# Low parts of six weight tiles formed by accumulating transfers, and one mean placed later, between the two layers of a hybrid encoder

## The chip, the core and the metric

The kernel runs on one core of a Trainium2 chip. The metric is the device time of one execution in microseconds (us). The core has a tensor engine (PE), VectorE (DVE), ScalarE (ACT), GpSimd (POOL) and a sync engine (SP) that issues most loads.

## The reference

Two layers of a bidirectional encoder over 512 tokens of 1024 channels, in float32. Each layer has two sub-layers, and each of these normalises its input and its output (RMS norm) and adds the output to the residual stream `x`:

```python
for l in range(DEPTH):                      # DEPTH = 2
    h = rms_norm(x, g_pre_mix[l])
    proj = h @ w_in[l]                      # 1024 -> 5632
    q_a, k_a, v_a, q_b, k_b, v_b, q_m, gate_pre = jnp.split(proj, splits, axis=-1)
    ...
    o_m = memory_attention(q_m, mem_n, w_mem_kv[l])   # keys and values: mem_n @ w_mem_kv[l]
    ...
    x = x + rms_norm(merged @ w_out[l], g_post_mix[l])
    h = rms_norm(x, g_pre_ffn[l])
    u = depthwise_conv_centred(h @ w_up[l], conv_w[l], conv_b[l])
    a, b = jnp.split(u, 2, axis=-1)
    x = x + rms_norm((jax.nn.gelu(a) * b) @ w_down[l], g_post_ffn[l])
```

`rms_norm(y, g)` is `y * rsqrt(mean(y*y) + 1e-6) * g`, the mean over the 1024 channels.

## The kernel before, in words

Channels lie on the 128 partitions, in `KD` = 8 groups; tokens lie along the free dimension, in two halves of 256 (`HALVES`). A float32 product is made of three matmuls in the type fp32r: each operand is split into a high part (a copy rounded to fp32r) and a low part (the operand minus its high part), and `mm3` (lines 249 to 254) adds high x high, weight high x operand low, and weight low x operand high. The weight's low part is thus wanted by the third of the three.

`weights` (lines 227 to 244) loads a weight tile of 128 output channels, 128x1024 elements or 512 KB, through SP into one of three buffers `wraw`. With a slot given, the tile is split in two chunks of 128x512: `split` (lines 223 to 225) lets ACT copy the chunk into the high part and lets the engine `eng` subtract that from the raw chunk into the low part. `eng` is VectorE (`V`) unless the caller names GpSimd (`G`). The buffer `wraw` is free when both have read it. The high and low parts of such tiles come from the pool of tiles called `m` (32 of them), so that in the profile ACT's copies read `m<-wraw` and the subtractions `m<-wraw,m`.

PE's order is written out by hand. `Woven` keeps a planner's clock that counts a cost for each matmul (a matmul of 256 columns counts 0.107 us), ties every PE instruction behind the one before, and holds a heap of jobs. A job is a generator: `yield t` makes it due again t us of the planner's clock later, `yield "flag"` parks it. `tick`, called after each step of `linear` or `run_group`, runs the jobs that are due, so the number in a `yield` decides behind how many matmuls the job's next PE instruction stands. `need(flag)` runs jobs until a flag is given.

Between the layers these things run side by side:

- `sublayer_end` of layer 0 (lines 815 to 862) ends the channel-mixing product for half 0, then for half 1. For half 0 it spawns `end_job` (lines 379 to 392): the reciprocal root of the mean square (`rstd_job`: PE multiplies the summed squares `acc` by the column `mean`, ACT takes the root, VectorE the reciprocal, PE transposes it back), then for each of eight channel groups `y = y * r`, `x = x + y`, and the squares of `x` summed into `acc2`. Then comes the next layer's `pre_norm_job`, which begins with the mean of `acc2` and writes the normalised tiles `h`.
- For half 1 it spawns `raw_end_job` (lines 418 to 445): the same, but each `x` is first split unnormalised (`raw`), so that PE can begin on it, and the mean of `acc2` (the yield of line 436 stands ahead of it) gives the factors `R`, by which the products are multiplied afterwards (lines 908 to 911), and the tiles `h` of half 1.
- `kv_ahead` (lines 1013 to 1023) loads and splits four key/value tiles of the next layer (`KVE`, line 38, names the engine for 1, 2 and 3) and the first two of the six tiles of the first projections (`GEN`, one letter for each of the six in `FIRST`). The other four follow at line 1029. `mem_kv` (lines 479 to 492) multiplies the key/value tiles; `run_group` (lines 501 to 514) multiplies the six tiles in three pairs, first by half 0, then by `raw`: the pairs' banks are called mm and mm, o and pt, s and s in the profile. Tiles 2 and 3 of the group (counted from 0) make the pair o and pt, tiles 4 and 5 the pair s and s.

With `KVE` = 'VVGG' and `GEN` = 'GGVGVG', six tiles are subtracted by GpSimd: key/value tiles 2 and 3, and tiles 0, 1, 3 and 5 of the group, in two chunks each.

GpSimd also runs, in this stretch, copies of the memory keys (`twice_split`), and for each attention head the load of its bias table and three subtractions (`a_bias`, lines 593 to 600). That load is tied behind `last_lo.get(G)`, the last low part that `split` gave to GpSimd.

Of the kernel before, what the change touches and what calls it, by code (L numbers as in the profile page):

```python
# [10 lines left out]
ALU = mybir.AluOpType  # L11
# [9 lines left out]
KD = D_MODEL // 128  # L21
# [6 lines left out]
FIRST = (0, 3, 4, 7, 6, 1)  # L28
# [6 lines left out]

LAT_QK, LAT_SM, LAT_T, LAT_V, LAT_T2 = 1.0, 4.5, 1.5, 2.0, 0.6
STEP_A, STEP_B, STEP_M = 9.0, 9.0, 5.5
SQG, LOG, GEN, KVE = {0: (), 1: ()}, {0: (), 1: ()}, 'GGVGVG', 'VVGG'
SD1 = 4.0
MARGIN = 0.3  # L40
SB = True
# [1 line left out]
KVD, GWD, NG, LAT1 = 7.3, 1.0, 2, 12.0  # L43
# [76 lines left out]
def tile_hybrid_encoder(ctx, tc, xT, memT, memg, vecs, rpb, w_in, w_kv, w_bra, w_brb, w_brm,  # L120
                        w_out, w_up, w_down, c_ident, c_mask, c_tab0, c_tab1, out):
    nc = tc.nc
# [13 lines left out]
    uid, last_copy, last_act, crit, last_lo = [0], [None], [None], [None], {}  # L136
    wv = Woven(tc)

    def nm(s):
        uid[0] += 1  # L140
        return f"{s}_{uid[0]}"


    def big(dt=F32R, shape=(128, 512)):
        return mp.tile(list(shape), dt, tag="m", name=nm("m"))
# [4 lines left out]
    def ktile(dt=F32R, shape=(128, 512)):  # L150
        return tp.tile(list(shape), dt, tag="ka", name=nm("ka"), bufs=12)
# [22 lines left out]
    def f32(ap):  # L174
        return ap.bitcast(F32)

    G = nc.gpsimd
    ACT, V = Counted(nc.scalar, wv, 0.1, 0.8e-3), Counted(nc.vector, wv, 0.065, 1.05e-3)

    DUP, MDUP = G, G  # L180
    MSQ = G

    def ready(least):
# [5 lines left out]
    def xh(k, half):  # L189
        return xs[:, half.start // 256, k, :]  # L190
# [27 lines left out]
    def behind(ins, other):  # L218

        if other is not None and ins is not other:  # L220
            tc.add_manual_dep(ins, other.name, ORDER, reason="issue order")

    def split(src, hi, lo, eng=None):
        last_copy[0] = ACT.copy(hi, src).ins
        last_lo[eng or V] = (eng or V).tensor_sub(lo, src, f32(hi)).ins

    def weights(src, K, C, slot=None, eng=None, after=None):

        raw = wp.tile([128, K, C], F32, tag="wraw", name=nm("wraw"))
        nc.sync.dma_start(out=raw, in_=src)  # L230
        if slot is None:
            hi = wp.tile([128, K, C], F32R, tag="whi", name=nm("whi"), bufs=2)
            lo = wp.tile([128, K, C], F32R, tag="wlo", name=nm("wlo"), bufs=2)
            split(raw, hi, lo, eng)
            behind(last_copy[0], after)
            return [(hi[:, k, :], lo[:, k, :]) for k in range(K)]
        n = 512 // C
        w = []
        for k in range(0, K, n):
            c = min(n, K - k)  # L240
            hi, lo = slot(F32R, (128, c, C)), slot(F32R, (128, c, C))
            split(raw[:, k:k + c, :], hi, lo, eng)
            w += [(hi[:, i, :], lo[:, i, :]) for i in range(c)]
        return w

# [68 lines left out]
    def sumsq_add(acc, src, first, slot=None, eng=None):  # L314
        if first:
            ACT.activation(acc, src, AF.Square)
        else:
            n = acc.shape[-1]
            sq = slot((128, 256)) if slot else small("sq2", 4) if n == 256 else small("sq", 1, (128, 512))
            ACT.activation(sq, src, AF.Square)  # L320
            (eng or V).tensor_add(acc, acc, sq)
# [4 lines left out]
    def rstd_job(accs, n, box):  # L326

        nb = n // 128
        bank = tbank((128, n + nb))
        pr, pt = bank[:, 0:n], bank[:, n:n + nb]  # L330
        for i, a in enumerate(accs):
            for b in range(nb):
                mm(pt[:, b:b + 1], a[:, 128 * b:128 * b + 128], mean, i == 0 and b == 0,
                   i == len(accs) - 1 and b == nb - 1, 0.11)
        rs = smalls(nb)
        crit[0] = ACT.activation(rs, pt, AF.Sqrt, bias=eps, scale=1.0).ins
        V.reciprocal(rs, rs)
        yield 0.8
        for b in range(nb):
            one = rs[:, b:b + 1]  # L340
            spread = bass.AP(one.tensor, one.offset, [list(one.ap[0]), [0, 128]])
            wv.pe(nc.tensor.transpose(pr[:, 128 * b:128 * b + 128], spread, ident), 0.11)
        box.append(pr)

    def normed(src, g, rs, hi, lo, eng=None):
        h32 = small("h32", 3)
        V.scalar_tensor_tensor(out=h32, in0=src, scalar=g, in1=rs, op0=ALU.mult, op1=ALU.mult)
        split(h32, hi, lo, eng)

    def raw_split(l, goff, k, src, hi, lo):  # L350

        g = vec[:, l, goff + k:goff + k + 1]
        ACT.activation(hi, src, AF.Copy, scale=g)
        V.scalar_tensor_tensor(out=lo, in0=src, scalar=g, in1=f32(hi), op0=ALU.mult, op1=ALU.subtract)

    def rtile():
        return tp.tile([128, 512], F32, tag="R", name=nm("R"), bufs=1)
# [60 lines left out]
    def raw_end_job(l, goff, og, acc, acc2, nxt, lat):  # L418


        half, box = HALVES[1], []
        hs, raw, R = nxt
        yield lat
        raw.extend((t[:, 0, :], t[:, 1, :]) for t in [ktile(F32R, (128, 2, 256)) for _ in range(KD)])
        yield from rstd_job([acc[:, half]], 256, box)
        for k in range(KD):
            V.tensor_mul(og[k][:, half], og[k][:, half], box[0])
            V.tensor_add(xh(k, half), xh(k, half), og[k][:, half])
            raw_split(l + 1, V_PRE, k, xh(k, half), *raw[k])
            if k == 0:  # L430
                yield 0.6
            wv.give(f"raw{k}")
            yield 1.05
        for k in range(KD):
            sumsq_add(acc2[:, half], xh(k, half), k == 0)
        yield 3.5
        box = []
        yield from rstd_job([acc2[:, half]], 256, box)
        ACT.copy(R[:, half], box[0])
        wv.give("R")  # L440
        for k in range(KD):
            normed(xh(k, half), vec[:, l + 1, V_PRE + k:V_PRE + k + 1], box[0], hs[k][0][:, half], hs[k][1][:, half])
        crit[0] = last_copy[0]
        yield 1.2
        wv.give(f"h{l + 1}.{V_PRE}.1")

    def h_tiles():
        return [(htile(), htile()) for _ in range(KD)]


    def mem_norm_job(l, hm, slot):
# [6 lines left out]
        for k in range(KD):  # L458
            sumsq_add(acc, raws[k], k == 0, None, MSQ if l else V)
        yield 14.0  # L460
# [34 lines left out]
    def group_weights(srcs, engs):  # L495
        return [weights(s, KD, 128, big, e) for s, e in zip(srcs, engs)]
# [19 lines left out]
    def proj(l, m, hs, after=None):  # L516
        w = weights(w_in[l, m], KD, 128, after=after)
        ps = mmbank()
        linear(ps, w, hs)
        return ps  # L520
# [366 lines left out]
    gw = group_weights([w_in[0, m] for m in FIRST[:2]], (V, V))  # L887
# [14 lines left out]
    for l in range(depth):  # L902
# [41 lines left out]
        for m in range(KD):  # L944
# [3 lines left out]
            hi, lo = big(), big()  # L948
# [4 lines left out]
        hs, R, gw = h_tiles(), rtile(), []  # L953
# [44 lines left out]
        if l == depth - 1:  # L998
            sublayer_end(l, V_POSTF, w_of, fs, 2, None)
            while wv.jobs:  # L1000
                wv._step()
        else:
            hm, km, vm = [], [], []
            wv.spawn(mem_norm_job(l + 1, hm, htile), 20.0)
            pre, R, raw, box = [], rtile(), [], []

            def then(a, i, l=l, box=box):
                box.extend(h_tiles())
                return pre_norm_job(l + 1, V_PRE, a, box, i)

            gw = []

            def kv_ahead(l=l, pre=pre, gw=gw):
                pre.append(weights(w_kv[l + 1, 0], KD, 128, htile))
                yield KVD
                for i in (1, 2, 3):
                    yield 0.9
                    pre.append(weights(w_kv[l + 1, i], KD, 128, big, G if KVE[i] == 'G' else V))
                wv.give(f"kv{l + 1}")
                for m in range(NG):  # L1020
                    yield GWD
                    gw.extend(group_weights([w_in[l + 1, FIRST[m]]], [G if GEN[m] == 'G' else V]))
                wv.give(f"gw{l + 1}")

            sublayer_end(l, V_POSTF, w_of, fs, 1, [then, (box, raw, R)], (1.4, LAT1), lambda: wv.spawn(kv_ahead()))
            wv.need(f"kv{l + 1}")
            mem_kv(l + 1, hm, km, vm, pre)
            wv.need(f"gw{l + 1}")
            gw += group_weights([w_in[l + 1, m] for m in FIRST[NG:]], [G if e == 'G' else V for e in GEN[NG:]])
            wv.need(f"h{l + 1}.{V_PRE}.0")  # L1030
            hs = box

# [92 lines left out]
```

## Time and profile before

| what | us |
|---|---|
| median of 3 runs | 1551.7 |
| lowest of them | 1549.61 |
| the profiled execution | 1551.73 |
| its span in the profile | 1550.0 |

The page of the profile gives busy times, the span in 40 slices, the DMA queues, the chain that ended last, and the costliest groups of instructions. The trace behind it was asked for waits, for timelines of one engine, for groups of one shape and for the granted clock of short stretches. Times of a timeline count from the span's start. A name such as `mm<-h,m` is output<-inputs, without buffer numbers; L114 is the helper through which all ACT and VectorE instructions pass, L247 the matmul of `mm`, L225 the subtraction of `split`, L342 the transposes of `rstd_job`.

### The profile page before, as it was taken

The page shows a single profiled execution, that of the slowest core. Times are in us where ns is not written, and L with a number is a line of the kernel's source. Part 1 is how long each engine was busy: PE and PEld are TensorE (multiplying, and loading weights), DVE is VectorE, ACT ScalarE, POOL GpSimd, SP SyncE. Part 2 cuts the span into 40 slices and gives each one's busy share as a digit, 9 for nine tenths or more (in the row PEclk, how much of TensorE's full clock was granted, in tenths as well). Part 3 has the DMA queues.
Part 4 walks back from the last instruction along what each step waited for, and adds up shares of the span by engine and source line. Part 5 has one row for each costly group of instructions (what it writes and reads, how often), then busy time and mean ns, then how long its engine had stood idle before and what let it go on. Part 6 is the DMA issues. An engine that isn't in the chain of part 4 may idle for free.

```text
span 1550.0 us, 20648 instructions
## 1 busy us (share of the span) xinstructions
PE 1522.5 (98%) x7970; PEld 1300.1 (84%) x7970; DVE 951.6 (61%) x1684; ACT 712.7 (46%) x1266; POOL 149.7 (10%) x217
## 2 busy tenths in 40 slices
PE   8999999999999999999989999999999999999997
PEld 7988888888988888888888888888889888888887
DVE  6685676335777777742497756753456977776233
ACT  5565554336544444532355555532354544444231
POOL 3340000110000000000154300002100000000000
PEclk9999999999999999999999999999999999999999
DMA  7221213235113322333431221132350233323331
GB/s 246 89 88 64 62 57 107 84 95 165 53 59 100 100 96 95 118 90 101 129 102 59 78 66 58 61 104 88 102 177 15 82 96 99 101 99 89 99 105 63
DMA packets 45810, 144.91 MB, mean 93 GB/s; under 512 B 5376, under 2 KB 9600, under 8 KB 45712
## 3 DMA queue, kind: packets, MB, share of 16 engines
q1 hardware_dynamic: 43776, 139.85, 28.5%
q10 hardware_dynamic: 1296, 2.10, 0.4%
q0 software_dynamic: 640, 1.64, 0.3%
q8 instruction: 62, 1.02, 0.3%
q14 instruction: 36, 0.29, 0.1%
HBM read 141.48 MB, written 2.10 MB: 93 GB/s over the span
## 4 chain that ended last, share of the span: by engine, by line
PE 91%; DVE 6%; ACT 2%; issue 1%; DMA 0%; SPq 0%; ACTq 0%; DVEq 0%
PE mm L247 80%; PE s L247 4%; PE o L247 3%; PE pt L258 2%; DVE m L114 1%; DVE y L114 1%; PE pt L247 1%; DVE ka L114 1%; DVE x L114 1%; ACT y L114 1%; DVE st L114 0%; DVE acc L114 0%; DMA x<-in_xT_dram 0%; DVE wlo L114 0%; ACT whi L114 0%
## 5 line engine op out<-in xcount | busy, mean ns | idle before, releaser
L247 PE MATMUL mm<-h,whi 128*128 128x512 f32 x2496 | 776.5, 392 | 0.0
L247 PEld LDWEIGHTS mm<-h,whi 128*128 128x128 f32 x2496 | 462.0, 188 | 91.3
L247 PE MATMUL mm<-h,wlo 128*128 128x512 f32 x1248 | 486.9, 390 | 0.0
L114 DVE TENSOR_TENSOR wlo<-wraw,whi 128x1024 fp32r<-128x1024 f32 (+1 forms) x213 | 259.2, 1217 | 284.7 <-ACT whi L114 282.3
L114 ACT CAST whi<-wraw 128x1024 fp32r<-128x1024 f32 (+1 forms) x213 | 221.4, 1040 | 307.8 <-PE mm L247 293.4
L247 PEld LDWEIGHTS mm<-h,wlo 128*128 128x128 f32 x1248 | 234.5, 188 | 49.6
L247 PE MATMUL mm<-m,whi 128*128 128x512 f32 (+1 forms) x800 | 215.1, 356 | 1.0 <-DVE m L114 0.8
L247 PEld LDWEIGHTS mm<-m,whi 128*128 128x128 f32 x800 | 141.8, 189 | 22.8 <-PE mm L247 1.3
L247 PE MATMUL mm<-m,wlo 128*128 128x512 f32 (+1 forms) x400 | 142.1, 355 | 0.0
L114 DVE SCALAR_TENSOR_TENSOR y<-y,vec,y 128x511 f32<-128x511 f32 x176 | 130.5, 748 | 3.5 <-ACT y L114 0.9
L114 DVE TENSOR_TENSOR y<-mm,R 128x512 f32<-128x512 f32 x82 | 56.4, 688 | 68.5 <-PE mm L247 68.5
L247 PEld LDWEIGHTS mm<-m,wlo 128*128 128x128 f32 x400 | 75.5, 189 | 10.9
L802 POOL TENSOR_TENSOR m<-m,y 128x512 f32<-128x512 f32 x28 | 36.1, 1289 | 399.4 <-DVE y L114 399.4
L114 ACT ACTIVATE y<-y,vec 128x512 f32<-128x512 f32 x88 | 71.1, 815 | 2.3 <-DVE y L114 1.9
L247 PE MATMUL mm<-m,m 128*128 128x512 f32 x240 | 63.5, 394 | 0.0
L114 ACT ACTIVATE y<-y 128x512 f32<-128x512 f32 x44 | 27.9, 633 | 71.7 <-DVE y L114 71.3
L114 ACT CAST m<-pt 128x512 fp32r<-128x512 f32 (+1 forms) x72 | 38.6, 541 | 46.8 <-PE pt L258 38.5
L114 ACT ACTIVATE y<-y,st 128x256 f32<-128x256 f32 (+1 forms) x80 | 43.8, 549 | 30.4 <-DVE st L114 28.9
L114 DVE TENSOR_TENSOR acc<-acc,sq 128x256 f32<-128x256 f32 (+1 forms) x80 | 41.1, 514 | 26.6 <-ACT sq L114 24.7
L114 DVE TENSOR_TENSOR m<-pt,m 128x512 fp32r<-128x512 f32 (+1 forms) x72 | 45.1, 630 | 19.9 <-ACT m L114 18.6
L114 ACT CAST m<-y 128x512 fp32r<-128x512 f32 x32 | 19.9, 622 | 72.5 <-DVE y L114 72.5
L247 PE MATMUL mm<-h,m 128*128 128x256 f32 x312 | 49.1, 301 | 2.0 <-ACT h L114 1.0
(154 smaller groups left out, 1789.9 us busy)
## 6 DMA issues: line engine op xcount, KB each, us to landing
wraw<-in_w_in_dram SPq DMA_DIRECT2D x88, 512.0 KB, 3.7
wraw<-in_w_up_dram SPq DMA_DIRECT2D x88, 512.0 KB, 3.6
wraw<-in_w_down_dram SPq DMA_DIRECT2D x32, 512.0 KB, 3.5
wraw<-in_w_out_dram SPq DMA_DIRECT2D x16, 512.0 KB, 3.9
wraw<-in_w_down_dram SPq DMA_DIRECT2D x16, 384.0 KB, 3.1
wraw<-in_w_kv_dram SPq DMA_DIRECT2D x8, 512.0 KB, 4.0
wraw<-in_w_bra_dram SPq DMA_DIRECT2D x16, 192.0 KB, 2.3
x<-in_xT_dram SPq DMA_DIRECT2D x8, 256.0 KB, 7.3
```

The source lines that it names most:

```text
L114: return op(*args, **kw)
L247: wv.pe(nc.tensor.matmul(ps, a, b, start=first, stop=last), cost)
L258: wv.pe(nc.tensor.transpose(ps[:, 128 * i:128 * i + 128], s, ident), 0.11)
L802: (V if br == 2 and m >= 6 else G).tensor_add(acc[m], acc[m], gs)
```

## The change

Six weight tiles get the letter 'D' in place of 'G'. For these, `weights` lets ACT copy the raw chunk into the high part as before; GpSimd multiplies the high part by -1 into the low part; and a DMA that GpSimd issues reads the same chunk of the weight from DRAM a second time and adds it to the low part where it lies (`accum_op=ALU.add`). The table `ENG` maps the letters. In `raw_end_job` the yield ahead of the mean of the second half's `acc2` is 5.0 instead of 3.5.

```diff
-SQG, LOG, GEN, KVE = {0: (), 1: ()}, {0: (), 1: ()}, 'GGVGVG', 'VVGG'
+SQG, LOG, GEN, KVE = {0: (), 1: ()}, {0: (), 1: ()}, 'DDVDVD', 'VVDD'
@@
     DUP, MDUP = G, G
+    ENG = {'G': G, 'V': V, 'D': 'D'}
@@ in weights()
             hi, lo = slot(F32R, (128, c, C)), slot(F32R, (128, c, C))
-            split(raw[:, k:k + c, :], hi, lo, eng)
+            if eng == "D":
+                last_copy[0] = ACT.copy(hi, raw[:, k:k + c, :]).ins
+                nc.gpsimd.tensor_scalar_mul(lo, f32(hi), -1.0)
+                nc.gpsimd.dma_start(out=lo, in_=src[:, k:k + c, :], accum_op=ALU.add)
+            else:
+                split(raw[:, k:k + c, :], hi, lo, eng)
@@ in raw_end_job()
         for k in range(KD):
             sumsq_add(acc2[:, half], xh(k, half), k == 0)
-        yield 3.5
+        yield 5.0
@@ in kv_ahead()
-                    pre.append(weights(w_kv[l + 1, i], KD, 128, big, G if KVE[i] == 'G' else V))
+                    pre.append(weights(w_kv[l + 1, i], KD, 128, big, ENG[KVE[i]]))
...
-                    gw.extend(group_weights([w_in[l + 1, FIRST[m]]], [G if GEN[m] == 'G' else V]))
+                    gw.extend(group_weights([w_in[l + 1, FIRST[m]]], [ENG[GEN[m]]]))
...
-            gw += group_weights([w_in[l + 1, m] for m in FIRST[NG:]], [G if e == 'G' else V for e in GEN[NG:]])
+            gw += group_weights([w_in[l + 1, m] for m in FIRST[NG:]], [ENG[e] for e in GEN[NG:]])
```

## Rows read from the trace of the kernel before

**Rows 1.** The page, part 1: busy us (share of the span) xinstructions.
```profile
PE 1522.5 (98%) x7970; PEld 1300.1 (84%) x7970; DVE 951.6 (61%) x1684; ACT 712.7 (46%) x1266; POOL 149.7 (10%) x217
```

**Rows 2.** Waits, 740 to 870 us: us in total, times, longest us.
```profile
PE pt L247 <- DVE acc L114: 4.6, 2, 3.5
```

**Rows 3.** Timeline of PE, 745 to 870 us: start, duration, what, [idle before <-releaser].
```profile
783.59 0.58 PE L247 MATMUL pt<-mean,acc 128*128 128x1 f32 x4 [3.46 <-DVE acc L114]
784.03 1.62 PE L247 MATMUL mm<-h,m 128*128 128x256 f32 x9
785.76 0.69 PE L342 MATMUL pt<-ident,st 128*128 128x128 f32 x2
786.10 4.79 PE L247 MATMUL mm<-h,m 128*128 128x256 f32 x30
```

**Rows 4.** The same timeline, from 795 us on.
```profile
795.53 0.43 PE L342 MATMUL pt<-ident,st 128*128 128x128 f32 x2
...
799.04 0.52 PE L247 MATMUL pt<-h,m 128*128 128x256 f32 x3
...
804.44 5.92 PE L247 MATMUL s<-h,m 128*128 128x256 f32 x48
...
813.64 0.58 PE L247 MATMUL pt<-mean,acc 128*128 128x1 f32 x4 [1.16 <-DVE acc L114]
```

**Rows 5.** Windows: length, busy us of five engines, PE's granted clock, DMA share, GB/s.
```profile
785.00:786.00 1.00, 0.90 (x5) 0.61 (x4) 0.67 (x3) 0.61 (x3) 0.93 (x3) 0.50 0.00 0
...
813.00:814.00 1.00, 0.36 (x4) 0.39 (x4) 0.42 (x1) 0.00 (x0) 0.94 (x3) 1.00 0.00 0
```

**Rows 6.** VectorE's groups, 769 to 784 us: busy us, mean ns | idle before.
```profile
L114 DVE TENSOR_TENSOR x<-x,y 128x256 f32<-128x256 f32 x8 | 6.7, 868 | 0.0
L114 DVE TENSOR_TENSOR acc<-acc,sq 128x256 f32<-128x256 f32 x8 | 5.1, 648 | 0.3 <-ACT sq L114 0.2
L114 DVE TENSOR_TENSOR y<-y,pt 128x256 f32<-128x256 f32 x8 | 3.0, 410 | 0.9 <-PE pt L342 0.9
```

**Rows 7.** Timeline of POOL, 745 to 890 us.
```profile
768.30 6.93 POOL L225 TENSOR_TENSOR m<-wraw,m 128x512 fp32r<-128x512 f32 x5 [105.56 <-ACT m L114]
776.61 4.24 POOL L225 TENSOR_TENSOR m<-wraw,m 128x512 fp32r<-128x512 f32 x3 [1.39 <-ACT m L114]
...
795.61 2.99 POOL L225 TENSOR_TENSOR m<-wraw,m 128x512 fp32r<-128x512 f32 x2 [8.35 <-PE s L258]
800.96 2.92 POOL L225 TENSOR_TENSOR m<-wraw,m 128x512 fp32r<-128x512 f32 x2 [2.36 <-ACT m L114]
...
808.18 2.62 POOL L599 TENSOR_TENSOR y<-mask,y 128x256 f32<-128x256 f32 x3 [3.79 <-DVE ka L114]
...
829.96 1.24 POOL L572 CAST ka<-zero 128x8 fp32r<-128x8 f32 x1
831.14 0.19 POOL L573 CAST ka<-zero 128x8 fp32r<-128x8 f32 x1
```

**Rows 8.** Timeline of VectorE, 786 to 832 us.
```profile
789.83 0.43 DVE L114 TENSOR_TENSOR h<-h,h 128x256 fp32r<-128x256 f32 x1 [0.98 <-ACT h L114]
...
816.41 1.26 DVE L114 SCALAR_TENSOR_TENSOR h<-x,vec,pt 128x256 f32<-128x256 f32 x3 [1.69 <-ACT R L114]
...
829.92 1.23 DVE L114 TENSOR_TENSOR wlo<-wraw,whi 128x1024 fp32r<-128x1024 f32 x1
```

**Rows 9.** POOL's groups, whole span: busy us, mean ns | idle before.
```profile
L802 POOL TENSOR_TENSOR m<-m,y 128x512 f32<-128x512 f32 x28 | 36.1, 1289 | 399.4 <-DVE y L114 399.4
...
L293 POOL CAST ka<-ka 64x512 fp32r<-64x512 f32 x12 | 7.5, 627 | 42.6 <-ACT ka L114 42.1
...
L596 POOL DMA_DIRECT2D y<-in_rpb_dram x12 | 6.7, 561 | 5.4 <-PE pt L258 5.4
```

**Rows 10.** Timeline of ACT, 794 to 802 us.
```profile
794.87 2.17 ACT L114 CAST m<-wraw 128x512 fp32r<-128x512 f32 x4
```

**Rows 11.** POOL's instructions on tiles y, 780 to 900 us: the bias loads.
```profile
DMA to landing us min/median/max: 2.3/2.8/4.2
```

**Rows 12.** The page, part 6: DMA issues, KB each, us to landing.
```profile
x<-in_xT_dram SPq DMA_DIRECT2D x8, 256.0 KB, 7.3
```

## The prediction

> **What bounds the kernel now.** I read the page first: the tensor engine (PE) is busy 98% of the span [rows 1]. So the only time to win is where PE stands still or runs slow, and what delays PE is paid almost one for one. I went on to the waits of the stretch between the layers. Two waits of one kind come to 4.6 us there: PE's mean (its product with the `mean` column) waits for VectorE's running sum `acc` [rows 2].
>
> The PE timeline shows the longer one and what it drags behind it [rows 3]. PE had nothing to do for 3.46 us before the mean of the first half at 783.59 us, so it arrived at 780.13. After that it is slow: from 784.03 to 790.89 us (786.10 + 4.79) it issues 39 matmuls of 256 columns and two transposes in 6.86 us. Later 48 such matmuls take 5.92 us and two transposes 0.43 us [rows 4], so 39 x 0.123 + 0.25 (the transposes overlap their neighbours) = 5.05 us would have done. The clock row says why: granted clock 0.50 at 785 to 786 us, that is 1.2 of 2.4 GHz [rows 5]. So this wait costs 3.46 + 1.8 = 5.3 us. The other, 1.16 us before the second half's mean at 813.64 [rows 4], is followed by a granted clock of 1.00 [rows 5]; it costs 1.16 us and no more.
>
> Why is `acc` late? Between 769 and 784 us VectorE adds `x<-x,y` in 868 ns and `acc<-acc,sq` in 648 ns on average, while `y<-y,pt` of the same shape, with one operand in PSUM, takes 410 ns [rows 6]. That is 8 x 0.46 + 8 x 0.24 = 5.6 us lost. In that stretch GpSimd (POOL) runs eight of its twelve subtractions, 6.93 + 4.24 = 11.2 us [rows 7]. That the two engines hold each other up shows at 829.96 in the same group: a POOL copy of 128x8 elements, 0.19 us in the row behind it, took 1.24 us, as long as VectorE's two-operand subtraction of 1.23 us that had begun at 829.92 [rows 8]. VectorE lost half of the time for which POOL held its operands.
>
> **The change part by part.** *POOL's work on the six tiles.* Twelve two-operand subtractions (6.93/5 = 1.4 us each) become twelve one-operand multiplies and twelve DMA issues. No multiply of this shape is in the trace. Bounds: a one-operand POOL copy of 512 columns takes 0.63 us, a two-operand add of 128x512 takes 1.29 us [rows 9]. I take 0.63, since the multiply reads one operand too. Eight multiplies hold 5.0 us instead of 11.2; with half of it lost as before, VectorE loses 2.5 us instead of 5.6, and `acc` comes 3.1 us earlier. PE's wait falls from 3.46 to about 0.35 us. At 1.29 us nothing is recovered; with a perfect fit all 3.46 us are. A POOL DMA issue costs 0.56 us [rows 9], so one chunk takes 1.2 us of POOL's queue, less than 1.4: POOL's later work (the copies of the keys, the bias) is not behind.
>
> The Trainium skill (GPSIMD Engine Reference, section 3.1) puts a lean one-input loop at 769 ns for 512 elements. No row here shows this multiply; by that figure, as an estimate, the loss is 3.1 us and the wait 0.95 us, and the sum below would be 0.6 us worse.
>
> *The clock.* A rest of 0.35 us is shorter than the 1.16 us after which the clock stayed at 1.00, so the 1.8 us should come back too, but not all of it: the transposes at 785.76 need a square root of ACT and a reciprocal of VectorE. At full clock PE is there 9 x 0.12 = 1.1 us after 784.03, at 785.1, and would wait up to 0.65 us. I count 1.15. Together 4.25 us (from 0 to 5.3).
>
> *The loads of the low parts.* Each low part is now complete only when an accumulating DMA of 256 KB has landed. For the two key/value tiles and tiles 0 and 1 of the group there is time: POOL's eighth subtraction begins near 779.4 (776.61 and two of 1.4 us), so its DMA is issued by 780.1, and between the mean (now near 780.5) and the group stand 48 matmuls, 5.8 us. Tile 3 is the tight one. ACT's four casts begin at 794.87 and take 2.17 us [rows 10], POOL follows the first at 795.61 [rows 7]. The multiply ends near 796.25, the DMA is issued at 796.3. PE meets tile 3 at 799.04 and wants its low part two matmuls later, at 799.28 [rows 4]; today's subtraction is done at 797.1. So the landing may take 3.0 us without harm. The trace has no accumulating transfer. POOL's loads of 128 KB land in 2.3 to 4.2 us, median 2.8 [rows 11]; the slowest loads of 256 KB take 7.3 us, at the kernel's start [rows 12]. Twice the bytes and a second stream to read make me take 3.5 us, nearest to the POOL rows: PE waits 0.5 us (0 to 4.3 us, and from a wait like that of [rows 3] the 1.8 us of a low clock too). The second chunk lands some 1.3 us later and is wanted four steps of six matmuls later, 2.9 us. Tile 5 starts at 800.96 [rows 7], lands at about 805.2, and is wanted five matmuls behind 804.44, at 805.05, plus the 0.5 us: free. The raw buffers come free one POOL operation earlier, which nobody waits for.
>
> The Trainium skill (DMA: Bandwidth & Descriptors, "Anatomy of one DMA") fits transfers that POOL issues as 2.0 us plus bytes over 436 GB/s, 2.6 us here as an estimate. No run here shows an accumulating one yet; by it tile 3 is in time and the sum is 0.5 us better.
>
> *The second half's mean.* The yield grows by 1.5 us of the planner's time. The order advances in steps of six matmuls, so two or three steps, 1.4 to 2.2 us, move in front of the mean. The 1.16 us wait is covered by matmuls that have to run anyway. `R` comes up to 1 us later in PE's order; its first reader on VectorE had idled 1.69 us before it [rows 8], so the engine has room to catch up, and the matmuls behind it are of other banks. I cost that at nothing; uncovered it would be 1 us. Gain 1.15 us (bounds 0 and 1.16); POOL's shorter holds might have removed that wait anyway, so it counts once.
>
> **Sum.** -4.25 - 1.15 + 0.5 = -4.9 us from the profiled execution's 1551.73 us (span 1550.0 and 1.7 around it, equal to the median of 1551.7): 1546.8 us. What follows is bound by PE and passes it on.
>
> **The rivals.** *The next chain is late instead.* PE gets to the second half's first transposes (795.53, [rows 4]) about 1.8 us earlier after the mean, but VectorE must first finish eight normalised tiles, and the reciprocal stands behind them. For: VectorE is busy there nearly without a break. Against: one of its gaps, 0.98 us [rows 8], waits for ACT, which itself stood behind slow matmuls. If 1.5 us are given back: 1548.3.
>
> *POOL's hold is no shorter* (a multiply at 1.29 us). The long wait and the slow clock stay, the second mean's 1.15 us is won, tile 3 comes 0.65 us later and costs 1.15: 1551.7, no change. Against: every one-operand row of POOL is shorter.
>
> *The accumulating transfers land late (slower than before).* One place decides, tile 3's first low part: each us of landing over 3.0 stops PE for one us, and a stop like that of [rows 3] adds the 1.8 us of the low clock. The gain without a stop is 5.4, so the break-even is 3.0 + 5.4 - 1.8 = 6.6 us of landing. At 7.3 us the time is 1551.73 - 5.4 + 4.3 + 1.8 = 1552.4; at 10 us 1555.1. For: two reads per written byte, and eight such transfers in a dozen us. Against: POOL's own loads are far from 6.6.
>
> *POOL's queue is reordered.* The bias load of the first head was tied behind POOL's last subtraction; the new path sets no such tie. If the load and its three subtractions, which now wait until 808.18 for VectorE [rows 7], came ahead of tile 5's multiply, that tile would land near 810.9 (three subtractions in 2.6 us behind 808.18) + 0.7 + 3.5 = 815.1 instead of by 805.2: about 10 us and the clock's 1.8, so some 1558.5 us. Against: the program still issues them later.
>
> **How the numbers follow.** Chances: forecast 0.45 (1545.3 to 1547.5), next chain late 0.2, no shorter hold 0.15, late landing 0.15, queue reordered 0.05. The lowest sum is 1551.73 - 5.3 - 1.16 = 1545.3, and I go a little below it for the spread of the runs (1549.6 and 1551.7). The range 1544.5 to 1554.0 leaves out the worst of the last two rivals. 2%, about what a measurement of this kernel can tell from no change, is 31 us; no case reaches it but transfers several times slower than any row: faster 0.01, same 0.97, slower 0.02.
>
> **What would show it.** Right: the first half's mean waits under 1 us, no clock row of 0.50 behind it, `x<-x,y` near 0.6 us, a POOL multiply near 0.65 us, no wait before the second half's mean, a wait of under 1 us at tile 3's first low part. Wrong: a multiply above 1 us, a landing above 5 us, or a new PE wait on VectorE between the two means.

## The result, and the profile after

The changed kernel took 1554.84 us (median; 1551.47 for the kernel before beside it), a ratio of 1.0025 with a 95% interval of 1.0019 to 1.0031. I had forecast 1546.8 us, 0.3% faster; it is 0.2% slower and just above the range.

PE's waits between the layers, 740 to 870 us, in the profile after (us in total, times, longest):

```profile
PE pt L253 <- DMA m<-in_w_in_dram: 5.2, 2, 2.8
...
PE pt L253 <- DVE acc L114: 2.3, 1, 2.3
...
PE pt L348 <- DVE st L114: 1.1, 2, 0.6
```

Of the two waits of [rows 2] one is left, shorter; two small ones for the reciprocal `st` are new, and two long ones for accumulating transfers. The timeline of PE shows where:

```profile
781.00 0.58 PE L253 MATMUL pt<-mean,acc 128*128 128x1 f32 x4 [2.25 <-DVE acc L114]
...
783.45 0.69 PE L348 MATMUL pt<-ident,st 128*128 128x128 f32 x2 [0.58 <-DVE st L114]
...
793.91 0.43 PE L348 MATMUL pt<-ident,st 128*128 128x128 f32 x2 [0.56 <-DVE st L114]
...
797.41 0.40 PE L253 MATMUL pt<-h,m 128*128 128x256 f32 x2
800.28 0.38 PE L253 MATMUL pt<-h,m 128*128 128x256 f32 x1 [2.47 <-DMA m<-in_w_in_dram]
...
803.01 0.40 PE L253 MATMUL pt<-h,m 128*128 128x256 f32 x2
806.18 0.39 PE L253 MATMUL pt<-h,m 128*128 128x256 f32 x1 [2.77 <-DMA m<-in_w_in_dram]
806.40 0.81 PE L253 MATMUL o<-h,m 128*128 128x256 f32 x3
...
819.35 0.50 PE L253 MATMUL pt<-mean,acc 128*128 128x1 f32 x4
```

Tile 3 (in the bank `pt`) issues two matmuls and stops at the third, the low part's, once for each of its two chunks: 2.47 and 2.77 us. The second stop is followed by the low clock; the window behind it (columns as in [rows 5]) has 0.50:

```profile
807.00:808.50 1.50, 1.50 (x8) 1.50 (x8) 1.50 (x2) 0.00 (x0) 1.50 (x3) 0.50 0.43 59
```

The second half's mean at 819.35 has no wait, where [rows 4] had 1.16 us.

To compare runs without what happens elsewhere in the kernel, I take the length of the stage from the start of key/value tile 1 to the start of the last pair's product with `raw` (`mm<-h,m` x24 and `s<-ka,m` x48 of PE's timeline): before 823.61 - 777.09 = 46.5 us, after 827.79 - 775.71 = 52.1. Of the 5.6 us the rows give: first mean -1.2, second mean -1.2, the two stops at tile 3 +5.2, the two waits for `st` +1.1, 18 matmuls from 806.40 to 810.05 at the low clock 3.65 instead of 2.16 us, +1.5. That is 5.4. (The medians differ by 3.4 us only, and the two profiled executions by 2.8. The profile after is 1.4 us shorter ahead of the stage, 775.7 against 777.1 us, and 1.4 us shorter behind it, 725.0 against 726.4. Behind it a stop of PE of 2.1 us is followed by the low clock before, and one of 1.6 us isn't after. Differences of this size come and go from profile to profile; the runs below show both.)

Why are the transfers late? POOL's timeline around tile 3, which answers to [rows 7]:

```profile
793.34 1.80 POOL L245 TENSOR_SCALAR m<-m 128x512 fp32r<-128x512 f32 x1
795.43 0.91 POOL L246 DMA_DIRECT2D m<-in_w_in_dram  x1 [0.30 <-POOL m L245]
796.07 1.82 POOL L245 TENSOR_SCALAR m<-m 128x512 fp32r<-128x512 f32 x1
797.51 0.91 POOL L602 DMA_DIRECT2D y<-in_rpb_dram  x1
798.20 1.15 POOL L246 DMA_DIRECT2D m<-in_w_in_dram  x1
798.78 2.22 POOL L245 TENSOR_SCALAR m<-m 128x512 fp32r<-128x512 f32 x1
802.63 0.83 POOL L605 TENSOR_TENSOR y<-mask,y 128x256 f32<-128x256 f32 x1 [1.63 <-DMA y<-in_rpb_dram]
803.41 0.89 POOL L246 DMA_DIRECT2D m<-in_w_in_dram  x1
```

The multiply takes 1.8 us, not 0.63; the issue takes 0.9 us, not 0.56, and begins 0.30 us behind the multiply's end. The bias load and a subtraction of the first head stand among the last four transfers. The landing of the transfer issued at 795.43 and of that at 798.20, asked one by one:

```profile
DMA to landing us min/median/max: 4.8/4.8/4.8
...
DMA to landing us min/median/max: 7.9/7.9/7.9
```

And beside the second, SP starts two loads of 512 KB:

```profile
798.59 0.80 SPq L231 DMA_DIRECT2D wraw<-in_w_in_dram  x2
```

VectorE, finally, 769 to 784 us, as in [rows 6]: `x<-x,y` is no faster than before, `acc` is.

```profile
L114 DVE TENSOR_TENSOR x<-x,y 128x256 f32<-128x256 f32 x8 | 7.1, 902 | 0.0
L114 DVE TENSOR_TENSOR acc<-acc,sq 128x256 f32<-128x256 f32 x8 | 4.1, 522 | 0.2 <-ACT sq L114 0.2
```

### The profile page after: what moved, and what is told of

It reads as the page before. It is cut to its first block, busy times and chain, and to the rows that moved or that the text cites. A ratio compares the mean times of both kernels' runs of the same rounds, so it can differ in the third digit from the quotient of the medians.

```text
span 1552.8 us, 20679 instructions
## 1 busy us (share of the span) xinstructions
PE 1520.9 (98%) x7970; PEld 1299.0 (84%) x7970; DVE 954.5 (61%) x1684; ACT 710.9 (46%) x1266; POOL 163.9 (11%) x229
## 4 chain that ended last, share of the span: by engine, by line
PE 91%; DVE 5%; ACT 2%; DMA 1%; issue 1%; POOL 0%; SPq 0%; ACTq 0%; POOLq 0%
PE mm L253 80%; PE s L253 5%; PE o L253 3%; PE pt L264 2%; DVE m L114 1%; DVE y L114 1%; PE pt L253 1%; DMA m<-in_w_in_dram 1%; ACT y L114 0%; DVE st L114 0%; DVE wlo L114 0%; DVE ka L114 0%; DMA x<-in_xT_dram 0%; DVE x L114 0%; ACT whi L114 0%
## 5 line engine op out<-in xcount | busy, mean ns | idle before, releaser
L114 ACT CAST m<-pt 128x512 fp32r<-128x512 f32 (+1 forms) x72 | 38.5, 540 | 45.1 <-PE pt L264 36.4
L114 DVE TENSOR_TENSOR m<-pt,m 128x512 fp32r<-128x512 f32 (+1 forms) x72 | 45.1, 629 | 18.9 <-ACT m L114 17.7
L114 DVE TENSOR_TENSOR m<-wraw,m 128x512 fp32r<-128x512 f32 (+1 forms) x58 | 38.1, 670 | 22.5 <-ACT m L114 22.5
```

What stands on the lines that cost most here:

```text
L114: return op(*args, **kw)
```

## The experiments

My theory after this: tiles 3 and 5, whose low parts are wanted soon after their copies, carry the loss, and the other two parts of the change help a little. The first four runs take the change apart by its letters and its yield.

**The mean alone.**

```diff
-... 'DDVDVD', 'VVDD'
+... 'GGVGVG', 'VVGG'
```

> All six tiles back to GpSimd's subtraction (letters of the kernel before), yield 5.0 kept. Theory (the loss comes from the tiles whose low parts are loaded): no wait before the second half's mean, everything else as in the kernel before, 1.2 us faster than it, about 1550.3. Rival (the later mean delays R and what is behind it): a new PE wait behind 829 us, time at or above 1551.5.

Measured: 1548.9 us, ratio 0.9991 (0.9983 to 1.0), stage 822.81 - 777.58 = 45.2 us, 1.3 less than before. The second mean has no wait, the first has 3.46 us as before, and no new wait appears behind the second. By the stage the later place is worth its 1.2 us, as forecast; the time agrees, but its interval reaches 1.0.

**The tiles alone.**

```diff
-        yield 5.0
+        yield 3.5
```

> Six tiles by accumulating transfers, yield 3.5 as before. Theory: same time as the changed kernel, 1554.8 within 0.5, because PE comes to the second mean some 5 us late anyway, so the wait of 1.16 us is gone without the yield. Rival (the two parts add up): the wait before the second mean is back and the time is 1556.0.

Measured: 1553.96 us, ratio 1.0027 (1.0017 to 1.0037), no wait at the second mean, and the stage at 50.8 us. So in the changed kernel the yield wins nothing: PE arrives there late anyway. The two parts don't add up.

**Early tiles only, late tiles only.**

```diff
-... 'DDVDVD', 'VVDD'
+... 'DDVGVG', 'VVDD'      (early)
+... 'GGVDVD', 'VVGG'      (late)
```

> Accumulating transfers only for key/value tiles 2 and 3 and group tiles 0 and 1; tiles 3 and 5 subtracted by GpSimd; yield 5.0. Theory: PE waits for no DMA in the group; the first mean still waits about 2 us; 1549.5 to 1551.0. Rival (the traffic and GpSimd's longer queue of the early tiles do the harm): GpSimd comes to tiles 3 and 5 late, PE waits over 2 us in the group, 1553 or more.

> Accumulating transfers only for group tiles 3 and 5, the four early ones subtracted by GpSimd; yield 5.0. Theory: PE waits for tile 3's first and second transfer, 2.5 us or more in sum, and the first mean waits 3.5 us as before; 1553.0 to 1556.0. Rival (the early tiles are the cause, by filling the queue): with that queue empty the transfers land within 3.5 us and the time is at or below 1551.0.

Measured: early 1547.93 us, ratio 0.9986 (0.9977 to 0.9994), stage 45.1; no wait for a transfer, 2.25 us at the first mean. Late 1555.04 us, ratio 1.0029 (1.0018 to 1.004), stage 50.2. PE's waits of the late run:

```profile
PE pt L253 <- DVE acc L114: 3.4, 1, 3.4
PE pt L253 <- DMA m<-in_w_in_dram: 3.2, 2, 2.1
```

The whole loss comes with tiles 3 and 5, both stops are at tile 3, and they are there with an empty queue before them: the two transfers land after 4.0 and 6.6 us. The early tiles do no harm. Whether they do good is open: the early run is 1.0 us below the run of the mean alone, but the intervals overlap, and the stages differ by 0.1 us.

Two things stay open: why the first mean still waits 2.25 us, and what makes tile 3's transfers late (the multiply, the order of POOL's queue, the accumulation, or SP's loads). The next runs each take one away.

**The tie put back.**

```diff
-                nc.gpsimd.dma_start(out=lo, ..., accum_op=ALU.add)
+                last_lo[G] = nc.gpsimd.dma_start(out=lo, ..., accum_op=ALU.add).ins
```

> The changed kernel with the tie put back: the accumulating DMA is noted in last_lo[G], so the first head's bias load (and its three subtractions) stand behind the last of the twelve. Theory A (the reordered queue makes tile 3's second transfer and tile 5's late): PE's second wait in the group, 2.8 us, and the low clock behind it shrink or go; 1552.0 to 1553.5 against 1554.8. Rival B (the transfers themselves are slow, the order costs nothing): second wait above 2 us still, time within 0.5 of 1554.8.

Measured: 1554.75 us, ratio 1.0025 (1.0015 to 1.0034), stage 50.5 us instead of 52.1. Four transfers now follow each other on POOL, and the bias load stands behind them. The stops at tile 3 are 2.25 and 0.78 us instead of 2.47 and 2.77:

```profile
802.38 0.39 PE L253 MATMUL pt<-h,m 128*128 128x256 f32 x1 [2.25 <-DMA m<-in_w_in_dram]
...
806.61 0.40 PE L253 MATMUL pt<-h,m 128*128 128x256 f32 x2
807.78 0.38 PE L253 MATMUL pt<-h,m 128*128 128x256 f32 x1 [0.78 <-DMA m<-in_w_in_dram]
```

That looks like theory A, but most of it has another reason. From the first stop to the second chunk PE takes 4.23 us here (802.38 to 806.61) and 2.73 in the profile after (800.28 to 803.01): in this run the low clock follows the first stop and not the second (granted clock 0.50 at 804 to 806 us, groups of three matmuls 0.84 us long instead of 0.52). PE comes 1.5 us later and so waits 1.5 us less. The run of the tiles alone, which has no tie, shows the same: 4.23 us, then a stop of 1.32. The second transfer is issued 2.75 us behind the first, against 2.77 without the tie, and lands after 7.2 us instead of 7.9. So the tie can have taken some 0.7 us of that stop at most, the transfer issued second is late without the reordering too, and on the time rival B is right.

**ACT writes the negative high part.**

```diff
-                nc.gpsimd.tensor_scalar_mul(lo, f32(hi), -1.0)
+                ACT.activation(lo, raw[:, k:k + c, :], AF.Copy, scale=-1.0)
```

> The changed kernel, the negative high part written by ACT (copy of the raw chunk with scale -1) instead of GpSimd's multiply; GpSimd only issues the twelve DMAs. Theory A (GpSimd's multiplies hold VectorE up and delay the transfers by 1.8 us each): x<-x,y falls from 0.90 to about 0.42 us, the first mean's wait below 0.5 us, tile 3's first wait below 1 us; 1547 to 1550. Rival B (the transfers and not the multiply are slow, and ACT's twelve extra copies delay the squares): waits for the transfers above 2 us, time 1552 or more.

Measured: 1550.87 us, ratio 0.9996 (0.9987 to 1.0005), stage 46.2. VectorE's groups of 769 to 784 us:

```profile
L114 DVE TENSOR_TENSOR acc<-acc,sq 128x256 f32<-128x256 f32 x8 | 3.4, 424 | 3.8 <-ACT sq L114 3.8
L114 DVE TENSOR_TENSOR x<-x,y 128x256 f32<-128x256 f32 x8 | 3.2, 422 | 0.0
```

Both are at the 410 ns of an undisturbed operation; the first mean waits 0.63 us, and the clock behind it is 1.00. This shows what held VectorE up: POOL's operations on SBUF operands, not its DMA issues, which are all still there. But tile 3 still stops PE for 2.16 us: its first transfer, now issued right behind ACT, lands after 5.1 us. Tile 1 and tile 5 stop it too, for 0.87 and 1.24 us. So the late tiles fail without any multiply, and the time can't be told from that of the kernel before.

**Plain loads instead of accumulating ones.**

```diff
-                nc.gpsimd.dma_start(out=lo, in_=src[...], accum_op=ALU.add)
+                nc.gpsimd.dma_start(out=lo, in_=src[...])
```

> The changed kernel with the twelve transfers as plain loads, without accumulation (the low parts are then the weights themselves, so this part of the computation is changed). Theory A (a landing is long because of the accumulation): median landing falls from 5.8 us to about 3.5 us and the first wait at tile 3 below 1.2 us. Rival B (GpSimd's descriptors and the queue set it): landing within 0.7 us of the changed kernel, the waits at tile 3 within 0.7 us of 2.5 and 2.8.

Measured: 1550.97 us, a single execution. All twelve landings (min/median/max):

```profile
DMA to landing us min/median/max: 2.8/3.9/6.6
```

against 3.7/5.8/7.9 after. An issue takes 0.6 instead of 0.9 us, and the first mean waits 1.15 us instead of 2.25. So accumulation costs about 2 us of the median landing here. Tile 3 still stops PE for 1.54 and 2.78 us, its second load landing after 6.6 us although nothing is added up. The answer lies between the two theories: accumulation for the median, something else for that one transfer.

**The raw buffers held.** The suspect is SP. With GpSimd no longer reading the raw chunk, its buffer is free when ACT has copied. In this stretch SP starts four loads: at 795.43, 798.63, 799.52 and 803.91 us before, and in two pairs at 793.81 and 798.59 after. Against the start of the stage the second and the fourth come 3.0 and 3.5 us earlier.

```diff
+    held_by = const.tile([128, 8], F32, name="held_by")
...
                 last_lo[G] = nc.gpsimd.dma_start(out=lo, ..., accum_op=ALU.add).ins
+                behind(nc.gpsimd.tensor_copy(held_by, raw[:, k, 0:8]).ins, last_lo[G])
```

> The tied kernel (bias load behind the last transfer), and each raw buffer held until its transfer is issued, by a copy of eight columns on GpSimd behind the DMA; so SP's next load of 512 KB starts later. Theory A (tile 3's second transfer lands late because SP's loads, released early, share the DMA engines): its landing falls from 7.2 us to 5.5 us or less, and PE's second wait in the group goes; the first wait stays near 2.2 us. Rival B (a second transfer is slow by itself, through GpSimd's multiply running behind it): landing stays within 0.7 us of 7.2.

Measured: SP's pair of loads, at 800.93 us in the tied run, 0.4 us behind tile 3's second transfer, starts later:

```profile
802.89 0.84 SPq L232 DMA_DIRECT2D wraw<-in_w_in_dram  x2
```

That transfer (issued at 801.67) and the next (804.63) land after

```profile
DMA to landing us min/median/max: 3.9/3.9/3.9
...
DMA to landing us min/median/max: 6.2/6.2/6.2
```

The long landing has moved with SP's loads to the next transfer, and PE's second stop in tile 3 is gone (though the low clock behind the first stop, 1.94 us, again brings PE there later). The eight early transfers show the same: in the tied run the two issued at 773.29 and 776.04, with a load of SP 0.5 us behind each, land after 6.6 and 7.6 us; here SP's loads begin 1.2 us behind a transfer, and all eight land within 4.5. Theory A is shown: loads of SP that begin close to a transfer lengthen its landing.

The time, 1556.2 us (ratio 1.0035, 1.0022 to 1.0049), is no better. With the twelve small copies the last early transfer is issued 1.1 us later than after, counted from the start of the stage, and PE is there 2.7 us earlier, since the first mean waits only 0.93 us and the clock behind it is 1.00. So tile 1's last transfer now stops PE for 2.41 us, with the low clock behind it. The short wait at the mean comes from VectorE, which loses less here to multiplies that are as long as after (769 to 784 us):

```profile
L114 DVE TENSOR_TENSOR acc<-acc,sq 128x256 f32<-128x256 f32 x8 | 4.7, 592 | 0.7 <-ACT sq L114 0.7
L114 DVE TENSOR_TENSOR x<-x,y 128x256 f32<-128x256 f32 x8 | 4.2, 544 | 0.0
```

**A copy instead of the multiply.**

```diff
-                nc.gpsimd.tensor_scalar_mul(lo, f32(hi), -1.0)
+                nc.gpsimd.tensor_copy(lo, f32(hi))
```

> The changed kernel with GpSimd's multiply by -1 replaced by GpSimd's copy of the high part (the low parts become high plus weight, so this part of the computation is changed). Theory A (the multiply is a slow form, a copy takes 0.63 us as the one-operand rows of before have it): the copy takes about 0.65 us, the first mean's wait falls below 1 us. Rival B (any one-operand GpSimd operation of 128x512 beside VectorE and a running transfer takes that long): 1.4 us or more, wait of 2 us.

Measured: 1551.38 us, a single execution. POOL's group, and VectorE's of 769 to 784 us:

```profile
L245 POOL CAST m<-m 128x512 fp32r<-128x512 f32 x12 | 10.4, 863 | 113.5 <-ACT m L114 106.7 <-issue 6.8
```

```profile
L114 DVE TENSOR_TENSOR acc<-acc,sq 128x256 f32<-128x256 f32 x8 | 6.4, 804 | 0.2 <-ACT sq L114 0.2
L114 DVE TENSOR_TENSOR x<-x,y 128x256 f32<-128x256 f32 x8 | 4.6, 589 | 0.0
```

Both theories are half right. The copy is short (0.86 us, 0.61 alone), so the multiply is a slow form, 1.83 us on average, longer than the subtraction of 1.4 us that it replaces. But the first mean waits 2.51 us all the same: VectorE loses 8 x (0.80 - 0.41) + 8 x (0.59 - 0.41) = 4.6 us to the 6.1 us that POOL's copies take from 769 to 784 us, three quarters of it and not half.

**Versions that win.** The early tiles with ACT's copy, tiles 3 and 5 by GpSimd; and the same with tile 1 by VectorE.

```diff
-... 'DDVDVD', 'VVDD'
+... 'DDVGVG', 'VVDD'      (and ACT's copy as above)
+... 'DVVGVG', 'VVDD'      (the second of them)
```

> Accumulating transfers for the four early tiles only, with ACT writing the negative high part; tiles 3 and 5 subtracted by GpSimd; yield 5.0. Theory (VectorE's lock was the price of the early tiles): x<-x,y about 0.42 us, no wait over 0.5 us at the first mean, no low clock behind it, 1545 to 1547, faster than the kernel before and than the run with GpSimd's multiply (1547.9). Rival (ACT's eight extra copies delay the squares): first mean's wait 2 us or more, 1548 or more.

> The early tiles with ACT's negative copy, but group tile 1 subtracted by VectorE (accumulating transfers for key/value tiles 2, 3 and group tile 0 only); tiles 3 and 5 by GpSimd; yield 5.0. Theory (with GpSimd's hold gone, ACT's copies and the queue of eight transfers are what is left): PE's waits at the first mean and for tile 1's transfer, 0.7 and 0.9 us, shrink; at or up to 1 us below the run with four early tiles. Rival (VectorE's two subtractions come ahead of acc): first mean's wait grows by 1 us or more.

Measured: 1545.07 us, ratio 0.9963 (0.995 to 0.9975), and 1544.57 us, ratio 0.9958 (0.9944 to 0.9971); both lie some 0.4% below the kernel before, clear of the intervals, and so below the changed one too. The difference between the two, 0.5 us, lies inside their intervals. In the first run the first mean waits 0.67 us, a little over the theory's 0.5. The eight transfers, issued close together, take 8.7 to 12.0 us to land; only one of tile 1's comes too late, by 0.87 us. In the second that wait is gone:

```profile
PE pt L253 <- DVE acc L114: 0.6, 1, 0.6
PE pt L348 <- DVE st L114: 0.2, 1, 0.2
```

The stage is 819.14 - 778.27 = 40.9 us there, 5.7 less than before: 2.9 at the first mean, 1.2 at the second, and the low clock of [rows 5] (1.3 us).

## Why the prediction was wrong

*What held.* The two waits, what the first drags behind it, and that POOL's hold on VectorE makes it: the runs without POOL's operations show each of these (x at 0.42 us, a wait of 0.6 us, the clock at 1.00). The second mean's 1.15 us was 1.2 to 1.3 in the run that has it alone; in the changed kernel the wait is gone with the old yield too, so there the yield earned nothing. Tile 3 was the tight one. Tile 5 stopped nothing, but by luck: tile 3 had held PE for 5.2 us, and in the run with ACT's copy tile 5 did stop it, for 1.24 us.

*The step that failed first* is "I take 0.63, since the multiply reads one operand too": the price of POOL's work. The multiply measured 1.83 us, above my upper end of 1.29, which I had from a two-operand add. A copy and a multiply are different POOL operations, and the nearest row by operand count was not the nearest by operation. With it fell "POOL is not behind": a chunk took some 2.75 us of its queue (769.44 to 772.24 and so on), not 1.2, and the last early transfer was issued at 788.08, not by 780.1. It fed the other terms: of my 3.1 us at the first mean 1.2 came, and the wait left, 2.25 us, kept a low clock behind it, so that of the 1.15 us of the clock 0.3 came and 1.1 us of waits for `st` were new.

*"Half of it lost as before"* came true in the changed kernel, but it is no rule. From 769 to 784 us VectorE lost 4.8 us there to 9.9 us of multiplies, but 4.6 to 6.1 with the copy, 3.6 to 9.5 with the plain loads, and 2.5 to 9.5 in the held run; the first mean waited 2.25, 2.51, 1.15 and 0.93 us. So the loss doesn't follow from the length of the hold, and by the copy's run even a multiply of 0.63 us need not have brought the 3.1 us. What sets the share stays open.

*"PE waits 0.5 us" at tile 3* is the term that turned the sign: the late tiles alone make the kernel slower. The first transfer was issued 2.4 us before PE stood at it, not 3.0, and landed after 4.8 us, not 3.5. The trace had no such transfer; the plain loads of the same size landed in 2.8 us at best, the accumulating ones in 3.6 to 4.0 with little beside them. The Trainium skill's fit (DMA: Bandwidth & Descriptors, "Anatomy of one DMA"), an estimate of 2.6 us, is near the plain one and low by 1.0 to 1.4 us for the accumulating one. The second transfer, which I put at nothing because it would land "some 1.3 us later", landed 5.9 us later: it was issued 2.8 us behind the first and took 7.9 us. It cost 2.77 us and 1.5 of low clock.

*"The raw buffers come free one POOL operation earlier, which nobody waits for"* is where that landing was lost from sight. Nobody waits for the buffer, but SP starts its next loads on it, and loads that begin close to a transfer lengthen its landing: 7.9 us with two of them 0.4 us behind it, and 3.9 in the held run with two 1.2 us behind. One of the pair stood near this place before as well, so how much of it the earlier release alone makes isn't shown. I had asked who waits and not what starts. The Trainium skill (DMA: Bandwidth & Descriptors, "Issuing engines are not separate DMA queues") says that transfers from different engines run on the same DMA engines and interleave; the moved loads of the held run agree.

*The rivals.* "The accumulating transfers land late" is what happened, at the place I named, but twice. "POOL's hold is no shorter" happened beside it: with 1.83 us a long wait and the low clock stayed. Of "the next chain is late instead" 1.1 us came, the two waits for `st`. "POOL's queue is reordered" happened as well, among the last four transfers, but tile 3's second transfer was issued no later for it, and the run without it was not faster.

## What to carry to other kernels

In this kernel low parts formed by accumulating transfers paid only for tiles that were wanted late: issued close together, eight of them landed after 8.7 to 12.0 us. For tiles 3 and 5, which are wanted soon after their copies, GpSimd's subtraction was better. Before an engine's operation is swapped for one with fewer operands, time that very operation: here the shorter-looking one was longer. And when a buffer's reader goes away, ask what its earlier release starts, not only who waits for it.

## What the runs showed of the hardware

- A GpSimd multiply by a constant of 128x512 elements took 1.57 us on average beside plain issues and 1.83 beside accumulating ones, a copy 0.6 to 0.95, a two-operand subtraction 1.4. The Trainium skill (GPSIMD Engine Reference, section 3.1) has 769 ns for 512 elements of a one-input loop at best: the copy lies about that figure, at its shortest below it, and the multiply takes twice the figure or more.
- An accumulating DMA issue of GpSimd is a row of 0.9 us, a plain one of 0.6; POOL's next operation begins some 0.6 us behind the start of either.
- An accumulating transfer of 256 KB landed in 3.6 to 4.0 us with little beside it, and in 6.6 to 7.9 when SP began two loads of 512 KB within 0.6 us of its issue (3.9 when they began 1.2 us behind it).
- GpSimd's DMA issues alone, without its operations on operands, left VectorE's additions at 0.42 us. With operations between them the additions took 0.41 to 1.5 us, and the share of POOL's time that VectorE lost was between a quarter and three quarters.
- PE's stops of 1.9 to 3.0 us were sometimes followed by the low clock and sometimes not. At tile 3's first chunk the matmuls behind 2.47 us kept their 0.12 us after, while behind 2.25 us in the tied run they didn't; at the first mean 2.25 us brought the clock of 0.50 after, and 2.51 us in the copy's run left it at 1.00. So which stop costs 1.5 us more can't be said from its length.
